# A hybrid decoder trunk on one core: the next block's x rows queued behind late weight loads, and the position bias spread by a copy inside DRAM in three separate hops

## The chip, the cores and the metric

The kernel runs on one core of one Trainium2 chip. The metric is the device time of one execution in microseconds (us). The time before is the median of three runs.

## The reference, cut to what matters

One decoder layer (DEPTH is 1) over 2048 positions of width 1024, in float32:

```python
h = _rmsnorm(x, norm_w[l])                  # needs the row sums of x*x
proj = h @ w_in[l]                          # one projection, columns split to three mixers
y_a = _hgrn2_branch(...)                    # A: gated linear recurrence
y_b = _gated_deltanet_branch(...)           # B: delta rule
y_c = _swa_sink_branch(c_q, c_k, c_v, c_g, sinks[l], bias_blk)   # C: windowed attention
lifted = jnp.einsum('bsnc,ncd->bsnd', ys, w_branch[l])
merged = jnp.sum(sigmoid(gate_logits) * lifted, axis=2)
x = x + merged @ w_out[l]
return _rmsnorm(x, final_norm)
```

`bias_blk` is a table of 128 queries by 256 keys for each of 8 heads. An entry depends on the distance of query and key alone, so one row of 384 values per head, read with a shift of one per query, gives the whole table.

## The kernel before

**Tiling.** `block(s)` treats 512 positions; there are four blocks, s = 0 to 3. Channels lie on the 128 partitions. Each block projects `h` (held as a high part `hH` and a low part `hL`, eight tiles of 128 channels each) with weights that are loaded anew: `load_w` (line 62) loads a 128x512 tile `wraw` by a DMA of SP's queue (L65), ACT rounds it to `wh` (L68), DVE takes the rest `wl` (L69), and `mm_ct` (line 74) does 12 matmuls with it (L80 to L82). Each of the three tiles has four buffers.

**Order of a block.** `unit_a(0)` to `unit_a(3)` (branch A, one head each), with `proj_k` among them; then `unit_b(0)` to `(3)`, with `merge(0)` among them; then `unit_c(0)`, `unit_c(1)`, `merge(1)`, then the norm of the next block, `unit_c(2)`, `unit_c(3)`, `merge(2)` and `output`. A `merge` gates and lifts one branch: 16 loads of `in_wct`, eight of `in_wb`. The units' small matmuls write banks `ps_c` of the tags c0 and c1 (two banks each), the projections banks `ps_d` (four).

**Who orders the work.** The Tile framework's planner puts each engine's instructions into one order ahead of the run: by priority, which is the order in the source, as soon as a planned instruction's inputs and buffers are free. At run time every engine works through its own order. All DMAs here are issued by SP, in one order too. `tc.issue_after(ins)` puts what is written under it behind `ins` on that instruction's own engine; it orders the issue and waits for nothing.

**The next block's norm.** `load_x` (line 102) loads one 128x512 part of `x` into `xs` (two buffers, L105) and ACT sums its squares (L107); eight such parts make a block. `norm_scale` (line 109) adds the sums and takes the power -0.5 on POOL (L111, L94, L95), then for each of four position tiles POOL makes a diagonal `dg` (L116) and PE spreads it to all partitions with `onesP` (L117) into a bank of c0; ACT copies the result to `R` (L119). In the source the loads of block s+1 stand behind `c1(yC)` of block s (lines 775 to 779). Nothing but the two `xs` buffers holds them back, so the planner put them early: at the start of block 0, and at the start of blocks 1 and 2.

**The position bias.** `bias_c` (line 250) is called once, behind `unit_a(0)` of block 0. It loads a table `onehot` (L252) and `relb` (L255), a matmul (L258) makes the row of 384 values for 8 heads on 8 partitions, DVE scales it to `rw` (L260). A DMA writes `rw` to DRAM 128 times, as `scr`, with heads outermost (L261: 8 x 128 x 384 values, 1536 KB). A second DMA reads `scr` with a shift of one value per partition into `bias8` (L263, 1024 KB). `bias8` is first used in `unit_c(0)` of block 0.

**Names in unit_a.** L345 to L348 make the gate `F` and the key `K` from the first projection; `silu2` (L99, L100) makes `Q` from the second; POOL multiplies `Q` and `K` to `prod` (L353), DVE then overwrites `Q` with `Q*F` (L354), which the first level's matmuls (L371) read; POOL makes the products `tots` of F over growing runs (L394).

Of the kernel before, what the change touches and what calls it, by code (L numbers as in the profile page):

```python
# [11 lines left out]
F32 = mybir.dt.float32  # L12
# [8 lines left out]
P = 128  # L21
# [3 lines left out]
NT = TB // P  # L25
# [5 lines left out]
RW = 384  # L31
# [7 lines left out]
def _trunk(tc, S, a, out):  # L39
    nc = tc.nc  # L40
# [6 lines left out]
    dram = ctx.enter_context(tc.tile_pool(name="dram", bufs=1, space=DRAM))  # L47
# [11 lines left out]
    def bank(tag="d", w=None):  # L59
        return ps.tile([P, 512], F32, name="ps_" + tag, tag=tag, bufs=4 if tag == "d" else 2)  # L60

    def load_w(src):
        n = src.shape[-1]
        raw = sb.tile([P, 512], F32, name="wraw", tag="wraw", bufs=WB)
        nc.sync.dma_start(raw[:, :n], src)  # L65
        wh = sb.tile([P, 512], F32R, name="wh", tag="wh", bufs=WB)
        wl = sb.tile([P, 512], F32R, name="wl", tag="wl", bufs=WB)
        A.copy(wh[:, :n], raw[:, :n])  # L68
        V.tensor_tensor(wl[:, :n], raw[:, :n], wh[:, :n].bitcast(F32), op=ALU.subtract)  # L69
        return wh[:, :n], wl[:, :n]  # L70

    last_mm, last_act = [None], [None]

    def mm_ct(p, src, rh, rl, nk):
        for q in range(nk // 4):
            wh, wl = load_w(src[q])
            for k4 in range(4):
                kt = 4 * q + k4
                ks = slice(k4 * P, (k4 + 1) * P)
                T.matmul(p, wh[:, ks], rh[kt], start=(kt == 0), stop=False)  # L80
                T.matmul(p, wh[:, ks], rl[kt], start=False, stop=False)  # L81
                last_mm[0] = T.matmul(p, wl[:, ks], rh[kt], start=False, stop=(kt == nk - 1)).ins  # L82
# [19 lines left out]
    def load_x(s, sq, i, tag="xs"):  # L102
        j, half = i // 2, i % 2
        t = sb.tile([P, TB], F32, name="xs", tag=tag, bufs=2)
        nc.sync.dma_start(t, a["x"][s * TB + j * P:s * TB + (j + 1) * P, half * TB:(half + 1) * TB])  # L105
        scrp = sb.tile([P, TB], BF16, name="scrp", tag="scrp", bufs=1)
        A.activation(scrp, t, AF.Square, accum_out=sq[:, j, half:half + 1])  # L107

    def norm_scale(sq):
        rs = sb.tile([P, NT], F32, name="rsx", tag="rsx")  # L110
        G.tensor_tensor(rs, sq[:, :, 0], sq[:, :, 1], op=ALU.add)  # L111
        rsq(rs, rs, 1.0 / D, EPS)
        rp = bank("c0")
        for j in range(NT):
            dg = sb.tile([P, P], F32, name="dg", tag="vn")
            G.tensor_tensor(dg, ident, rs[:, j:j + 1].broadcast_to([P, P]), op=ALU.mult)  # L116
            T.matmul(rp[:, j * P:(j + 1) * P], onesP, dg, start=True, stop=True)  # L117
        R = sb.tile([P, TB], F32, name="R", tag="R", bufs=1)
        A.copy(R, rp)  # L119
        return rs, R  # L120
# [15 lines left out]
    def mm_tc(src, n, lh, ll, step=1, each=None, tags=("d", "d", "d", "d")):  # L136
        pj = [bank(t) for t in tags]
        for k0 in range(0, KT, step):
            w = []
            for kt in range(k0, k0 + step):  # L140
                if each:
                    each(kt)
                w.append(load_w(src[kt]))
            for j in range(NT):
                js = slice(j * P, (j + 1) * P)
                for kt in range(k0, k0 + step):
                    wh, wl = w[kt - k0]
                    T.matmul(pj[j][:, :n], lh[kt][:, js], wh, start=(kt == 0), stop=False)  # L148
                    T.matmul(pj[j][:, :n], lh[kt][:, js], wl, start=False, stop=False)  # L149
                    T.matmul(pj[j][:, :n], ll[kt][:, js], wh, start=False, stop=(kt == KT - 1))  # L150
        return pj
# [95 lines left out]

    bias8 = const.tile([P, 8, 256], F32, name="bias8", tag="bias8")

    def bias_c():  # L250
        onehot = sb.tile([33, RW], F32, name="onehot", tag="tr", bufs=2)
        nc.sync.dma_start(onehot, a["onehot"])  # L252
        relb = const.tile([33, 8], F32, name="relb", tag="relb")
        G.memset(relb, BIG)
        nc.sync.dma_start(relb[0:32, :], a["relb"])  # L255
        scr = dram.tile([P, 8, RW], F32, name="scr", tag="scr")
        pb = bank("c0")
        T.matmul(pb[0:8, :RW], relb, onehot, start=True, stop=True)  # L258
        rw = sb.tile([8, RW], F32, name="rw", tag="tr", bufs=2)
        V.tensor_scalar(rw, pb[0:8, :RW], 8.0, None, op0=ALU.mult)  # L260
        nc.sync.dma_start(scr.rearrange("p h w -> h p w"), rw.rearrange("h (o w) -> h o w", o=1).broadcast_to([8, P, RW]))  # L261
        skew = bass.AP(tensor=scr.tensor, offset=scr.offset + 127, ap=[[8 * RW - 1, P], [RW, 8], [1, 256]])
        nc.sync.dma_start(bias8, skew)  # L263

    halo = const.tile([P, 12, 3], F32, name="halo", tag="halo")
    G.memset(halo, 0.0)
# [16 lines left out]
    def block(s, hH, hL, last=None):  # L283
# [342 lines left out]
        def proj_k():  # L626
            pk = proj_ct(32)
            for g in range(2):
                r = slice(g * 64, g * 64 + 64)
                if s > 0:  # L630
                    for t in (kH[g], kL[g]):
                        G.tensor_copy(t[:, 0:P], t[:, TB:TB + P].bitcast(F32))
                for r2 in (r, slice(64 - g * 64, 128 - g * 64)):
                    A.copy(kH[g][r2, P:], pk[r, :])
                    V.tensor_tensor(kL[g][r2, P:], pk[r, :], kH[g][r, P:].bitcast(F32), op=ALU.subtract)
# [109 lines left out]
        yA = new_y()  # L745
        f0 = unit_a(0)
        if s == 0:
            bias_c()
        f1 = unit_a(1)
        f0(yA)  # L750
        proj_k()
        f2 = unit_a(2)
        f1(yA)
        f3 = unit_a(3)
        with tc.issue_after(last_act[0]):
# [18 lines left out]
        c1(yC)  # L774
        if s + 1 < NSB:
            sq = sb.tile([P, NT, 2], F32, name="sqx", tag="sqx")
            for i in range(2 * NT):
                load_x(s + 1, sq, i)
            R = norm_scale(sq)[1]
        unit_c(2)(yC)  # L780
        unit_c(3)(yC)
# [5 lines left out]
    for s in range(NSB):  # L787
        hs_ = block(s, *hs_)
# [88 lines left out]
```

## Time and profile before

| | us |
|---|---|
| median of three runs | 2551.77 |
| lowest and highest | 2550.91, 2551.85 |
| the profiled execution, whole | 2551.53 |
| its span, first to last instruction | 2549.7 |

The profiled execution is 0.24 us under the median, and 1.83 us of it lie outside its span. TensorE (PE) is busy for 97% of the span, DVE for 58%, ACT for 45%, POOL for 19%, and the 16 DMA engines for about a third of it. A busy figure is a mean over stages; the stages differ, and what a change in one of them is worth is read from that stage.

A block takes about 628 us, and block 0 has a start of some 45 us ahead of it. PE's clock has two levels in the records, 1.2 and 2.4 GHz; a stretch's granted clock is the mean share of full speed, so 0.83 over 10 us means that 3.4 of them ran at half speed.

### The profile page before, as it was taken

What the parts mean: (1) busy time and instruction counts of PE and PEld (TensorE: products, weight loads), DVE (VectorE), ACT (ScalarE), POOL (GpSimd) and SP (SyncE); (2) the same over time, 40 slices, a digit from 0 to 9 for tenths busy, and PEclk for the clock granted to TensorE, in tenths of its full rate; (3) what the DMA queues carried; (4) which work ended last, traced back from release to release, by engine and by line L of the source; (5) the groups of instructions that cost most, each with busy time, mean ns of one, the idle gap of its engine ahead of it and who ended that gap; (6) DMA issues with size and microseconds to landing.
All of it is one profiled execution on the core that took longest, in us unless ns stands there. A gap on an engine that the chain in (4) does not pass through costs nothing.

```text
span 2549.7 us, 39021 instructions
## 1 busy us (share of the span) xinstructions
PE 2464.3 (97%) x13658; PEld 1945.7 (76%) x13658; DVE 1487.5 (58%) x3706; ACT 1151.0 (45%) x2806; POOL 472.0 (19%) x821
## 2 busy tenths in 40 slices
PE   8899998999999999899999999989999999998998
PEld 7677776778977777677887777767788787776876
DVE  5566566555467657555536666664554676666443
ACT  6354344343545434435444643443434463444343
POOL 3221111211222201120222311111121221111112
PEclk9999999999999999999999999989999999999999
DMA  7423331224522233122452223212344223221233
GB/s 218 79 90 83 84 89 43 66 83 151 164 67 69 78 84 86 43 77 88 147 151 59 78 80 86 80 35 87 91 127 127 63 78 82 84 74 49 83 108 95
DMA packets 162265, 229.97 MB, mean 90 GB/s; under 512 B 49379, under 2 KB 60548, under 8 KB 162068
## 3 DMA queue, kind: packets, MB, share of 16 engines
q1 hardware_dynamic: 162068, 227.47, 31.3%
q8 instruction: 108, 1.77, 0.3%
q14 instruction: 89, 0.73, 0.1%
HBM read 214.53 MB, written 12.88 MB: 89 GB/s over the span
## 4 chain that ended last, share of the span: by engine, by line
PE 87%; DVE 4%; DMA 4%; ACT 2%; POOL 1%; issue 1%; SPq 0%; POOLq 0%; DVEq 0%; ACTq 0%
PE ps_d L80 21%; PE ps_d L81 21%; PE ps_d L82 20%; PE ps_d L149 3%; PE ps_d L148 3%; PE ps_d L150 3%; PE ps_c L371 2%; PE ps_c L701 2%; DMA wraw<-in_wct_dram 1%; PE ps_c L692 1%; DMA scrX<-L 1%; PE ps_c L516 1%; PE ps_c L570 1%; DMA XB<-scrX 1%; DVE wl L69 1%
## 5 line engine op out<-in xcount | busy, mean ns | idle before, releaser
L80 PE MATMUL ps_d<-hH,wh 128*128 128x512 f32 x1952 | 790.8, 405 | 12.3 <-DVE mm L669 5.9
L82 PE MATMUL ps_d<-hH,wl 128*128 128x512 f32 x1952 | 796.4, 408 | 0.1
L68 ACT CAST wh<-wraw 128x512 fp32r<-128x512 f32 (+1 forms) x712 | 429.1, 604 | 812.5 <-PE ps_d L81 659.1
L81 PE MATMUL ps_d<-hL,wh 128*128 128x512 f32 x1952 | 792.0, 406 | 0.0
L69 DVE TENSOR_TENSOR wl<-wraw,wh 128x512 fp32r<-128x512 f32 (+1 forms) x712 | 487.9, 687 | 409.8 <-ACT wh L68 400.0
L80 PEld LDWEIGHTS ps_d<-hH,wh 128*128 128x128 f32 x1952 | 370.9, 190 | 93.2 <-DVE mm L669 6.5
L82 PEld LDWEIGHTS ps_d<-hH,wl 128*128 128x128 f32 x1952 | 370.9, 190 | 79.2 <-issue 1.7
L81 PEld LDWEIGHTS ps_d<-hL,wh 128*128 128x128 f32 x1952 | 370.7, 190 | 79.0 <-issue 0.9
L331 POOL TENSOR_TENSOR msum<-msum,gth 128x512 f32<-128x512 f32 x64 | 104.7, 1638 | 452.1 <-DVE gth L330 452.1
L80 PE MATMUL ps_d<-yH,wh 128*128 128x512 f32 x384 | 154.8, 405 | 3.9 <-ACT yH L311 3.3
L81 PE MATMUL ps_d<-yL,wh 128*128 128x512 f32 x384 | 158.0, 412 | 0.5 <-DVE yL L312 0.5
L82 PE MATMUL ps_d<-yH,wl 128*128 128x512 f32 x384 | 158.1, 412 | 0.0
L148 PE MATMUL ps_d<-wh,mH 128*128 128x512 f32 x256 | 100.1, 391 | 0.0
L149 PE MATMUL ps_d<-wl,mH 128*128 128x512 f32 x256 | 100.0, 391 | 0.0
L150 PE MATMUL ps_d<-wh,mL 128*128 128x512 f32 x256 | 99.9, 390 | 0.0
L471 DVE SCALAR_TENSOR_TENSOR qkB<-raw,convw,qkB 128x512 f32<-128x512 f32 x96 | 71.6, 746 | 29.2 <-ACT qkB L469 28.4
L80 PEld LDWEIGHTS ps_d<-yH,wh 128*128 128x128 f32 x384 | 72.5, 190 | 20.8 <-ACT yH L311 4.1
L81 PEld LDWEIGHTS ps_d<-yL,wh 128*128 128x128 f32 x384 | 73.1, 190 | 19.1 <-DVE yL L312 2.3
L82 PEld LDWEIGHTS ps_d<-yH,wl 128*128 128x128 f32 x384 | 73.1, 190 | 15.3 <-issue 0.3
L330 DVE SCALAR_TENSOR_TENSOR gth<-gth,ps_d 128x512 f32<-128x512 f32 x64 | 43.7, 685 | 68.0 <-PE ps_d L82 67.8
L371 PEld LDWEIGHTS ps_c<-qk 128*64 128x64 f32 x1536 | 53.3, 139 | 38.8 <-issue 20.5
L221 POOL TENSOR_TENSOR soB<-soB,eq 128x1 f32<-128x1 f32 x64 | 15.1, 236 | 346.4 <-ACT junkB L618 346.3
(281 smaller groups left out, 3813.1 us busy)
## 6 DMA issues: line engine op xcount, KB each, us to landing
wraw<-in_wct_dram SPq DMA_DIRECT2D x488, 256.0 KB, 2.6
wraw<-in_wb_dram SPq DMA_DIRECT2D x96, 256.0 KB, 2.6
wraw<-in_wo_dram SPq DMA_DIRECT2D x64, 256.0 KB, 2.6
wraw<-in_wtc_dram SPq DMA_DIRECT2D x64, 162.0 KB, 2.8
xT<-in_xT_dram SPq DMA_DIRECT2D x32, 256.0 KB, 4.2
xs<-in_x_dram SPq DMA_DIRECT2D x32, 256.0 KB, 4.2
rt<-in_x_dram SPq DMA_DIRECT2D x32, 256.0 KB, 3.3
out_dram<-rt SPq DMA_DIRECT2D x32, 256.0 KB, 2.6
```

The lines of the kernel that those rows point to most:

```text
L68: A.copy(wh[:, :n], raw[:, :n])
L69: V.tensor_tensor(wl[:, :n], raw[:, :n], wh[:, :n].bitcast(F32), op=ALU.subtract)
L80: T.matmul(p, wh[:, ks], rh[kt], start=(kt == 0), stop=False)
L81: T.matmul(p, wh[:, ks], rl[kt], start=False, stop=False)
L82: last_mm[0] = T.matmul(p, wl[:, ks], rh[kt], start=False, stop=(kt == nk - 1)).ins
L148: T.matmul(pj[j][:, :n], lh[kt][:, js], wh, start=(kt == 0), stop=False)
L149: T.matmul(pj[j][:, :n], lh[kt][:, js], wl, start=False, stop=False)
L150: T.matmul(pj[j][:, :n], ll[kt][:, js], wh, start=False, stop=(kt == KT - 1))
L331: G.tensor_tensor(m, m, th, op=ALU.add)
L371: T.matmul(sp[g * 64:g * 64 + 64, c * 32:(c + 1) * 32], K[:, c * P + g * 64:c * P + g * 64 + 64], qv[:, c, g * nb // 2:(g + 1) * nb // 2, ...
L471: V.scalar_tensor_tensor(dst, raw[:, j:j + TB], convw[:, ti, j:j + 1], dst, op0=ALU.mult, op1=ALU.add)
L701: T.matmul(ob[hh * 64:hh * 64 + 64, ci * P:(ci + 1) * P], cv_[:, c + b, hh * 64:hh * 64 + 64], pts[ci][:, hh, b, :], start=(b == b0), stop ...
```

## The change

The x rows of the next block are issued behind the weight load written last before them, which is the last one of `merge(1)`. `bias_c` is cut into three: `bias_rows` writes `rw` once to DRAM as `rowd` (12 KB); `bias_spread`, behind `unit_a(1)`, copies `rowd` 128 times to `scr`, from DRAM to DRAM, with the 128 copies outermost and 12 KB in each; `bias_load`, behind `unit_a(2)`, reads the shifted table as before. Each hop is put behind the weight load that was written last.

```diff
     def load_w(src):
...
-        nc.sync.dma_start(raw[:, :n], src)
+        last_ld[0] = nc.sync.dma_start(raw[:, :n], src).ins
...
-    last_mm, last_act = [None], [None]
+    last_mm, last_act, last_ld = [None], [None], [None]
...
-    def bias_c():
+    rowd = dram.tile([8, RW], F32, name="rowd", tag="rowd")
+    scr = dram.tile([P, 8 * RW], F32, name="scr", tag="scr")
+
+    def bias_rows():
         onehot = sb.tile([33, RW], F32, name="onehot", tag="tr", bufs=2)
         nc.sync.dma_start(onehot, a["onehot"])
         relb = const.tile([33, 8], F32, name="relb", tag="relb")
         G.memset(relb, BIG)
         nc.sync.dma_start(relb[0:32, :], a["relb"])
-        scr = dram.tile([P, 8, RW], F32, name="scr", tag="scr")
         pb = bank("c0")
         T.matmul(pb[0:8, :RW], relb, onehot, start=True, stop=True)
         rw = sb.tile([8, RW], F32, name="rw", tag="tr", bufs=2)
         V.tensor_scalar(rw, pb[0:8, :RW], 8.0, None, op0=ALU.mult)
-        nc.sync.dma_start(scr.rearrange("p h w -> h p w"), rw.rearrange("h (o w) -> h o w", o=1).broadcast_to([8, P, RW]))
+        with tc.issue_after(last_ld[0]):
+            nc.sync.dma_start(rowd, rw)
+
+    def bias_spread():
+        with tc.issue_after(last_ld[0]):
+            nc.sync.dma_start(scr, rowd.rearrange("h (o w) -> o (h w)", o=1).broadcast_to([P, 8 * RW]))
+
+    def bias_load():
         skew = bass.AP(tensor=scr.tensor, offset=scr.offset + 127, ap=[[8 * RW - 1, P], [RW, 8], [1, 256]])
-        nc.sync.dma_start(bias8, skew)
+        with tc.issue_after(last_ld[0]):
+            nc.sync.dma_start(bias8, skew)
...
         f0 = unit_a(0)
         if s == 0:
-            bias_c()
+            bias_rows()
         f1 = unit_a(1)
+        if s == 0:
+            bias_spread()
         f0(yA)
         proj_k()
         f2 = unit_a(2)
+        if s == 0:
+            bias_load()
...
         c1(yC)
         if s + 1 < NSB:
             sq = sb.tile([P, NT, 2], F32, name="sqx", tag="sqx")
-            for i in range(2 * NT):
-                load_x(s + 1, sq, i)
+            with tc.issue_after(last_ld[0]):
+                for i in range(2 * NT):
+                    load_x(s + 1, sq, i)
             R = norm_scale(sq)[1]
```

## Rows read from the trace of the kernel before

**Rows 1.** The page: each engine's busy us, share of the span, instructions.

```profile
PE 2464.3 (97%) x13658; PEld 1945.7 (76%) x13658; DVE 1487.5 (58%) x3706; ACT 1151.0 (45%) x2806; POOL 472.0 (19%) x821
```

**Rows 2.** PE's waits over the span: us in total, times, longest.

```profile
PE ps_c L117 <- POOL dg L116: 5.4, 4, 1.9
PE ps_d L80 <- ACT wh L68: 4.1, 1, 4.1
PE ps_c L371 <- DVE qk L354: 3.7, 1, 3.7
```

**Rows 3.** SP's timeline, 75 to 185 us: start, length, then what was issued.

```profile
92.14 0.30 SPq L261 DMA_DIRECT2D scr<-rw  x1
94.30 20.30 SPq L65 DMA_DIRECT2D wraw<-in_wct_dram  x4
```

**Rows 4.** The chain that ended last, 90 to 130 us: start, length, what.

```profile
94.30 31.31 DMA wraw<-in_wct_dram
```

**Rows 5.** PE's timeline, 119 to 131 us; in brackets the idle time before and its releaser.

```profile
126.30 0.60 PE L80 MATMUL ps_d<-hH,wh 128*128 128x512 f32 x1 [4.14 <-ACT wh L68]
126.70 0.63 PE L81 MATMUL ps_d<-hL,wh 128*128 128x512 f32 x1
```

**Rows 6.** Stretches: length, busy time by engine, granted clock, DMA share, GB/s.

```profile
60.00:70.00 10.00, 6.26 (x39) 4.92 (x38) 3.41 (x6) 5.59 (x12) 5.75 (x11) 0.93 0.44 147
70.00:80.00 10.00, 10.00 (x84) 7.04 (x84) 5.84 (x15) 0.62 (x1) 0.00 (x0) 0.73 0.30 81
...
120.00:130.00 10.00, 5.86 (x19) 4.09 (x18) 2.72 (x4) 4.27 (x7) 2.43 (x8) 0.83 0.70 192
...
1030.00:1090.00 60.00, 50.45 (x270) 36.73 (x270) 37.82 (x137) 23.64 (x65) 7.92 (x17) 0.91 0.15 37
...
2286.00:2346.00 60.00, 49.26 (x278) 35.75 (x277) 41.85 (x143) 26.74 (x75) 8.00 (x12) 0.97 0.16 41
...
1280.00:1330.00 50.00, 49.69 (x282) 45.15 (x281) 18.91 (x42) 27.29 (x64) 9.24 (x22) 1.00 0.58 170
```

**Rows 7.** Tile xs, 25 to 66 us: count, ns least/median/most, first to last start.

```profile
L105 SPq DMA_DIRECT2D xs<-in_x_dram x10: 327/328/430, 29.5 to 63.0; - x10
...
L107 ACT ACTIVATION_READ_ACCUMULATOR scrp<-xs x8: 186/187/193, 34.5 to 62.8; 128x1 f32 x8
```

**Rows 8.** POOL's timeline, 58 to 70 us.

```profile
61.97 2.86 POOL L394 TENSOR_TENSOR tots<-tots 128x128 f32<-128x128 f32 x6
65.04 0.20 POOL L111 TENSOR_TENSOR rsx<-sqx 128x4 f32<-128x4 f32 x1 [0.21 <-issue]
...
66.62 1.26 POOL L353 TENSOR_TENSOR prod<-qk 128x512 f32<-128x512 f32 x1
```

**Rows 9.** ACT's timeline, 48 to 70 us.

```profile
55.85 0.63 ACT L107 ACTIVATE scrp<-xs 128x512 bf16<-128x512 f32 x1 [1.34 <-DMA xs<-in_x_dram]
...
59.41 0.60 ACT L345 ACTIVATE F<-ps_d 128x512 f32<-128x512 f32 x1
...
63.38 0.59 ACT L99 ACTIVATE th<-ps_d 128x512 f32<-128x512 f32 x1
```

**Rows 10.** PE's timeline, 64 to 70 us.

```profile
64.61 0.40 PE L82 MATMUL ps_d<-hH,wl 128*128 128x512 f32 x1
68.75 1.07 PE L371 MATMUL ps_c<-qk 128*64 128x32 f32 x16 [3.74 <-DVE qk L354]
```

**Rows 11.** DMAs by kind: line engine op xcount, KB each, median us to landing.

```profile
xs<-in_x_dram SPq DMA_DIRECT2D x32, 256.0 KB, 4.2
...
LT<-gscr SPq DMA_DIRECT2D x16, 256.0 KB, 3.3
```

**Rows 12.** SP's timeline, 484 to 530 us, end of merge(1) in block 0.

```profile
495.43 0.33 SPq L65 DMA_DIRECT2D wraw<-in_wb_dram  x1
498.23 25.53 SPq L65 DMA_DIRECT2D wraw<-in_wct_dram  x10
```

**Rows 13.** PE's timeline, 526 to 529 us: the scores of unit_c(2).

```profile
528.16 0.28 PE L663 MATMUL ps_c<-kH,qs 128*128 128x256 f32 x1
```

## Prediction

> **What bounds the kernel now.** The page comes first: PE is busy for 2464.3 of 2549.7 us [rows 1]. So only three things can move the time much: a gap of PE, a stretch in which PE's clock is at its lower level, or another order of PE's work. I therefore read PE's waits next. Nearly all are short and come back in every block; two are single and long: 4.1 us for a rounded weight, and 3.7 us for `Q*F` [rows 2]. Both lie in the first 130 us, and the change touches what stands ahead of each.
>
> The first: SP issues the write of `scr` at 92.14, and from 94.30 four weight loads behind it [rows 3]. The chain shows a weight load from 94.30 on its way for 31.31 us [rows 4], and PE runs dry 4.14 us before 126.30 [rows 5]. So the write of 1536 KB took some 31 us, 51 GB/s, and the loads that share its queue ended with it. When PE starts again it is at half speed: 0.60 and 0.63 us for matmuls that take 0.40 elsewhere, and a granted clock of 0.83 over 10 us [rows 5, 6, 10].
>
> The second: PE ends its third projection at 65.0 and waits 3.74 us for L354 [rows 10]. POOL is what is late: it ends `tots` at 64.83, then does three norm instructions of block 1, and only at 66.62 `prod` [rows 8], which L354 must await. The norm waits for ACT's squares of x rows; ten row loads are in those first 65 us [rows 7]. So the early rows put 1.8 us into POOL's order, and squares into ACT's ahead of `F` [rows 8, 9]. PE's clock is 0.93 and 0.73 in the two stretches of 10 us around it [rows 6].
>
> **The change part by part.** The sums are against the profiled execution, 2551.53 us, of which 1.83 lie outside the span and don't change; the median is 0.24 higher.
>
> *The bias in three hops.* Removed is the 1536 KB write from eight partitions; added are a 12 KB write, a copy of 1536 KB inside DRAM and one more wait of SP. No copy inside DRAM is in the trace. From below: at the best rate of the stretches shown, 192 GB/s [rows 6], 1536 KB take 8.2 us. From above: six times a broadcast of one DRAM row to 256 KB, at 3.3 us to landing [rows 11], 20 us. I take 10, nearer the lower end, since each of the 3.3 us has a start and an end in it that one copy has once. Loads behind the copy land later by up to that. The load of 94.30 was needed when PE ran dry, at 126.30 - 4.14 = 122.2 [rows 5], less 0.6 for rounding (the size of ACT's step in [rows 9]), so it may take 27 us, and either end fits. The gap goes: -4.1 us. With it goes the slow stretch behind it, 10 x (1 - 0.83) = 1.7 us [rows 6]. SP's added wait, of the 12 KB write to landing, is at most the 3.3 us of a load twenty times its size [rows 11], within the same 27; only weight loads are queued behind it. `bias_load` is the same DMA as before, one unit later; SP again holds loads behind its wait for `scr`, and `bias8` isn't needed before `unit_c(0)`, at the end of branch B. Sum: -5.8 us; between 0 (the cover doesn't reach) and -5.8.
>
> Here the Trainium skill speaks against the step. By "DMA: Bandwidth & Descriptors", section "Rules for kernel authors", an outermost dimension of fewer than 16 confines a DMA to as many engines. By that the old write sat on 8 of them, and the new copy, with 128 outermost, sits on all 16, so that no part of a weight load can pass it. The 51 GB/s of the old write agree; no run here shows the copy yet. The same page's section "Specifications" gives about 358 GB/s of HBM for a core; reading and writing 1536 KB would by that be an estimate of 8.8 us, and the sum is the same.
>
> *The x rows at the start of block 0.* Ten loads of 256 KB leave (block 1's eight and two of block 2's [rows 7]), with eight squares of 0.63 us on ACT [rows 9] and POOL's three norm steps. `prod` needs `Q`: `th` ends at 63.97 [rows 9], DVE's step on it is one of at most 0.87, which is all that lies between the end of `prod` and PE's start [rows 8, 10]; so 64.8, and POOL is free of `tots` at 64.83. With the norm gone `prod` starts at 64.9, 1.75 us earlier, and the gap would still be 2.0. But `F`, `tots` and `th` move too: ahead of `F` ACT waited 1.34 us for an x row, behind a square stands another, and more stand before `th` [rows 9]. If `F` comes 2 to 3 us earlier, `prod` can start at about 62.0 to 62.5 and PE 1.26 + 0.87 later, at 64.1 to 64.6, before the third projection ends at 65.0 [rows 8, 10]. So the gap lies between 0 and 2.0. I take 0, since the square of [rows 9] waited for its x row, and `F` stood in ACT's order behind it. Gain: 3.7 us, and with the gap its slow stretch, 10 x (0.07 + 0.27) = 3.4 us [rows 6]. Sum: -7.1; between -1.8 (POOL's part alone, and the clock falls as now) and -7.1. What is late next is PE itself, which has projections to do.
>
> *The x rows at the start of blocks 1 and 2.* PE is busy for 49.69 of 50 us there [rows 6], so what leaves costs it little: 0 to 1 us in all. I take -0.5.
>
> *The norm in its new place.* The rows now leave behind the load of 495.43 (block 0; the others lie one block apart), in a stretch in which SP loads one projection weight each 2.8 us, ten in 28 us [rows 12], and each pays for 12 matmuls. Eight issues of SP, and on ACT eight squares of 0.63 + 0.19 [rows 7, 9], 6.6 us, beside a share of 45% over the span [rows 1]; nothing by itself. L117 waits for `dg` 5.4 us in four places now, the longest, 1.9, in the start of block 0, which stays [rows 2]; the other three cost 3.5 in sum and leave the end of branch B. In the new place PE reaches L117 with the same POOL steps ahead of it: 0 to 1.9 a block. I take 1.2 each, the mean of those three: net 0; between -3.5 and +2.2.
>
> *The clock in branch C.* The 60 us there have 0.91 in block 1 and 0.97 in block 3, with much the same work but for the norm [rows 6]: 60 x 0.06 = 3.6 us that hang on where short gaps fall. The change shifts them all. I take 0; up to 3.6 us either way in a block, and, as they won't all fall alike, 6 in all.
>
> Sum: -5.8 - 7.1 - 0.5 + 0 = -13.4; 2551.5 - 13.4 = 2538.1 us, its own range 2531 to 2545.
>
> **The rivals.**
> *The start stays half late* (0.14). Only POOL's 1.75 us come off, because `F` waited for PE's first projection and not for ACT's squares, which the trace doesn't tell apart, and the clock still falls: -5.8 - 1.8 - 0.5, so 2543.4.
> *The copy takes the old write's place* (0.08). If it takes over 27 us, or the planner puts it where SP's lead over PE is shorter, PE runs dry as before: -7.1 - 0.5, so 2543.9; with the start half late too, 2549.
> *Nothing that counts moves* (0.09). The planner orders the block anew once x rows aren't ready early; PE's gaps come back at other lines and eat the gain: 2548 to 2554. For it speaks that the two long waits are only 8 us of 85 in which PE idles; against it, that both have a named cause that goes.
> *More than the two gaps* (0.08). The norm takes branch C's gaps and slow stretches along, as block 3 lacks them: 3 x (1.2 + 2.1) more, 2528.
> *The norm comes too late* (0.06), slower than before. R's bank is one of the two c0 banks that `unit_c(2)` needs for its third score matmul, at 528.16 [rows 13]. The last of eight rows is issued at 495.8 + 7p, where p is the pace that SP's order and the two `xs` buffers allow; then 4.2 to land [rows 11], 0.6 for the square, 1.6 for the norm's steps on POOL [rows 8] and 1.9 for `dg` and L117, as its longest wait [rows 2]. That is 504.1 + 7p, in time up to p = 3.4. One row per weight load is p = 2.8, in time by 4 us. At p = 4.5 PE waits 7.5 us in each of three blocks, +22, and the time is 2560. It decides against the change from 3.4 + (13.4 / 3) / 7 = 4.0 us a row.
> The forecast keeps 0.55.
>
> **How the numbers follow.** A change under 0.2%, 5.1 us, can't be told from none here, so faster means under 2546.7: all of the forecast and of "more", nine tenths of the half late start, half of the slow copy, 0.80. Slower is the late norm and a little of "nothing", 0.07. The rest, 0.13, is the same. For 8 in 10 I leave out the late norm, half of "nothing" and what lies under 2526: 2526 to 2551.
>
> **What would show it.** Right, if PE's waits have no row of L80 for L68 and none of L371 over 1 us in the first 130 us, if the stretch from 60 to 80 us has a granted clock of 1.00, if weight loads behind the copy land within 20 us, and if L105 stands behind the last `in_wb` load of `merge(1)`, with L117 in the projections that follow. Wrong, if PE waits over 2 us at L117 or L663 near 500 to 530 us of a block, or if SP's waits show L65 held behind L105 while PE idles for `wh`.

## The result, and the profile after

The changed kernel takes 2525.29 us (median of four, 2522.55 to 2526.73) beside 2551.34 (four, 2545.85 to 2551.85): ratio 0.9896, 95% interval 0.9881 to 0.9911. That is 26 us less, where 13.4 were forecast, and just under the low end of the range, 2526. Four more executions in a later set gave 2525.87 beside 2549.39 (0.991, interval 0.9893 to 0.9928), 23.5 less. The direction and both named causes were right; about half of the gain was not in the sum.

The profiled execution of the changed kernel took 2523.94 us, 2522.2 of it span. Lines behind the bias functions are 10 higher in it (L371 is L381, L353 is L363, L307 is L317). The page's engine totals, as in [rows 1]:

```profile
PE 2450.0 (97%) x13658; PEld 1936.2 (77%) x13658; DVE 1488.5 (59%) x3706; ACT 1153.1 (46%) x2806; POOL 475.8 (19%) x821
```

PE does the same 13658 matmuls in 14.3 us less, and is idle for 72.2 us where it was idle for 85.4. So of 27.5 us of span, 13.2 were idle time and 14.3 were busy time. Most of the latter is clock: span x (1 - granted clock) fell by 13.0, from 33.1 (0.987) to 20.2 (0.992). The forecast had 8.3 of idle time and 5.1 of clock.

PE's waits (total, times, longest) have no row of L80 for L68 and none of L381; of L117 and L317 they say:

```profile
PE ps_c L317 <- ACT LT L315: 6.2, 4, 1.6
...
PE ps_c L117 <- POOL dg L116: 1.8, 3, 1.1
```

L117 fell from 5.4 [rows 2], and L317 rose: it was 3.7 us as L307 of the kernel before. SP's timeline from 75 to 130 us shows the three hops:

```profile
81.42 0.30 SPq L264 DMA_DIRECT2D rowd<-rw  x1
83.58 0.33 SPq L65 DMA_DIRECT2D wraw<-in_wct_dram  x1
83.95 0.58 SPq L268 DMA_DIRECT2D scr<-rowd  x1
86.88 9.47 SPq L65 DMA_DIRECT2D wraw<-in_wct_dram  x2
96.44 0.39 SPq L273 DMA_DIRECT2D bias<-scr  x1
```

The DMAs by kind (count, KB, us to landing) have the copy, and ACT's timeline has the rounding of the load issued behind it at 86.88:

```profile
scr<-rowd SPq DMA_DIRECT2D x1, 1536.0 KB, 8.6
```

```profile
93.33 0.62 ACT L68 CAST wh<-wraw 128x512 fp32r<-128x512 f32 x1 [0.71 <-PE ps_d L81]
```

The copy took 8.6 us, 183 GB/s, where the old write of the same bytes took some 31: [rows 4] show a load queued behind it, and its own packets ran from 93.0 to 124.6. ACT waited for a buffer that PE had to leave, not for the load. Stretches at the start of block 0, with columns as in [rows 6]:

```profile
60.00:70.00 10.00, 10.00 (x108) 7.25 (x107) 6.56 (x17) 1.74 (x3) 0.00 (x0) 1.00 0.30 85
70.00:80.00 10.00, 10.00 (x77) 7.59 (x76) 6.23 (x16) 6.34 (x16) 4.36 (x13) 1.00 0.18 50
...
120.00:130.00 10.00, 10.00 (x119) 7.34 (x116) 8.02 (x20) 3.63 (x9) 0.00 (x0) 1.00 0.16 48
```

PE is full and at its upper clock where it had 0.93, 0.73 and 0.83. POOL (first fence) has no norm step between `tots` and `prod` [rows 8]; `prod` ends at 58.50, and PE (second fence) goes from its third projection to L381 without a gap, at 60.91 instead of 68.75 [rows 10]:

```profile
54.08 2.79 POOL L404 TENSOR_TENSOR tots<-tots 128x128 f32<-128x128 f32 x6
57.20 1.30 POOL L363 TENSOR_TENSOR prod<-qk 128x512 f32<-128x512 f32 x1 [0.33 <-DVE qk L100]
```

```profile
60.59 0.39 PE L82 MATMUL ps_d<-hH,wl 128*128 128x512 f32 x1
60.91 0.66 PE L381 MATMUL ps_c<-qk 128*64 128x32 f32 x16
```

In its new place the norm is in time. SP issues eight rows from 474.59 to 487.6, 1.9 us a row, behind the last `in_wb` load of `merge(1)`; PE takes the four `dg` (L117, eight instructions) within projections. In block 0, shown here, no wait is over 0.1; in blocks 1 and 2 the longest is 0.32, and the three blocks' waits listed above sum to 0.6, for 3.5 before:

```profile
474.21 0.33 SPq L65 DMA_DIRECT2D wraw<-in_wb_dram  x1
474.59 0.90 SPq L105 DMA_DIRECT2D xs<-in_x_dram  x2
...
485.84 2.12 SPq L105 DMA_DIRECT2D xs<-in_x_dram  x2
```

```profile
495.27 0.61 PE L117 MATMUL ps_c<-dg,onesP 128*128 128x128 f32 x4
495.63 0.47 PE L80 MATMUL ps_d<-hH,wh 128*128 128x512 f32 x1
496.19 0.85 PE L117 MATMUL ps_c<-dg,onesP 128*128 128x128 f32 x4
```

**Where the 27.5 us of span lie.** From PE's timeline I take four milestones: the first projection of `hH`, the first matmul of branch B's inversions that reads `X` and `NS`, the first score matmul of branch C, and the first matmul of `output()`. Lengths in us:

| stretch | before | after | change |
|---|---|---|---|
| start to first projection of hH | 47.7 | 43.0 | -4.7 |
| block 0, to branch B | 182.2 | 170.4 | -11.8 |
| block 0, branch C to output | 222.2 | 219.1 | -3.1 |
| block 1 and 2, start to branch B | 240.7, 242.1 | 240.6, 240.7 | -1.5 |
| block 1 and 2, branch C to output | 219.65, 219.95 | 217.3, 217.3 | -5.0 |
| branch B of blocks 0 to 2 | 500.2 | 499.7 | -0.5 |
| block 3 and the end | 675.0 | 674.1 | -0.9 |

The second row holds both forecast gaps, and there the forecast (4.1 + 1.7 + 3.7 + 3.4 = 12.9) was nearly right. The head (-4.7) was in no step, and branch C (-8.1 in this pair) was put at 0. The stretches of branch C, before (first fence) and after; the second column is the length, the third PE's busy time, and the granted clock is third from the end:

```profile
396.60:618.80 222.20, 208.48 (x1027) 161.53 (x1028) 117.50 (x318) 91.99 (x232) 34.51 (x39) 0.96 0.27 77
1026.40:1246.00 219.60, 209.08 (x1052) 162.83 (x1053) 119.11 (x318) 94.08 (x232) 34.99 (x40) 0.97 0.27 78
```

```profile
380.00:599.00 219.00, 207.53 (x1027) 160.68 (x1028) 118.74 (x318) 97.65 (x248) 36.74 (x42) 0.97 0.30 88
1006.30:1223.60 217.30, 206.06 (x1052) 160.36 (x1053) 119.57 (x318) 98.96 (x248) 37.89 (x43) 0.98 0.30 88
```

In block 1 PE's idle time rose by 0.7 us (10.5 to 11.2) and its busy time fell by 3.0 with the same 1052 instructions: there the gain of branch C is clock. In block 0, 2.2 of the 3.1 us were idle time (13.7 to 11.5). What this pair shows does not hold for all traces, as the experiments tell.

The head hangs on POOL. Timelines of POOL before (first fence) and after (second):

```profile
22.97 0.38 POOL L94 TENSOR_SCALAR rsx<-rsx 128x4 f32<-128x4 f32 x1
28.83 0.31 POOL L356 MEMSET ST<- 64x256 f32 x1 [5.48 <-DMA scrX<-zb]
29.22 1.03 POOL L95 TENSOR_TENSOR rsx<-rsx,mhalf 128x4 f32<-128x4 f32 x1
30.33 0.76 POOL L116 TENSOR_TENSOR dg<-ident,rsx 128x128 f32<-128x128 f32 x2
```

```profile
20.61 0.38 POOL L94 TENSOR_SCALAR rsx<-rsx 128x4 f32<-128x4 f32 x1
21.08 1.38 POOL L95 TENSOR_TENSOR rsx<-rsx,mhalf 128x4 f32<-128x4 f32 x1
22.54 1.11 POOL L116 TENSOR_TENSOR dg<-ident,rsx 128x128 f32<-128x128 f32 x2
27.60 0.31 POOL L366 MEMSET ST<- 64x256 f32 x1 [3.96 <-DMA scrX<-zb]
27.99 0.76 POOL L116 TENSOR_TENSOR dg<-ident,rsx 128x128 f32<-128x128 f32 x2
```

In the kernel before, the norm of block 0 stood behind a memset of `ST` (unit_a's, line 356) that waits until the zeros of `zb` have gone to `scrX`; in the changed kernel the planner put that memset behind half of the norm. R is copied 4.5 us after the memset before and 1.7 us after it now (33.30 to 28.83, 29.32 to 27.60). No line of the change touches this memset.

### The profile page after: what moved, and what is told of

It reads as the page before. It is cut to its first block, busy times and chain, and to the rows that moved or that the text cites. A ratio compares the mean times of both kernels' runs of the same rounds, so it can differ in the third digit from the quotient of the medians.

```text
span 2522.2 us, 39006 instructions
## 1 busy us (share of the span) xinstructions
PE 2450.0 (97%) x13658; PEld 1936.2 (77%) x13658; DVE 1488.5 (59%) x3706; ACT 1153.1 (46%) x2806; POOL 475.8 (19%) x821
## 4 chain that ended last, share of the span: by engine, by line
PE 90%; DVE 4%; DMA 2%; ACT 2%; issue 1%; POOL 1%; SPq 0%; POOLq 0%; DVEq 0%; ACTq 0%
PE ps_d L80 21%; PE ps_d L81 21%; PE ps_d L82 21%; PE ps_d L148 3%; PE ps_d L149 3%; PE ps_d L150 3%; PE ps_c L381 2%; PE ps_c L711 2%; PE ps_c L702 1%; DMA scrX<-L 1%; PE ps_c L526 1%; PE ps_c L580 1%; DMA XB<-scrX 1%; PE ps_c L623 1%; PE ps_c L614 1%
## 5 line engine op out<-in xcount | busy, mean ns | idle before, releaser
L80 PE MATMUL ps_d<-hH,wh 128*128 128x512 f32 x1952 | 787.7, 404 | 8.2 <-DVE mm L679 5.9
L68 ACT CAST wh<-wraw 128x512 fp32r<-128x512 f32 (+1 forms) x712 | 429.2, 604 | 798.2 <-PE ps_d L81 621.5
L80 PEld LDWEIGHTS ps_d<-hH,wh 128*128 128x128 f32 x1952 | 368.8, 189 | 88.0 <-DVE mm L679 6.5
L80 PE MATMUL ps_d<-yH,wh 128*128 128x512 f32 x384 | 155.9, 408 | 4.1 <-ACT yH L321 3.7
L148 PE MATMUL ps_d<-wh,mH 128*128 128x512 f32 x256 | 99.9, 390 | 0.0
L80 PEld LDWEIGHTS ps_d<-yH,wh 128*128 128x128 f32 x384 | 72.8, 191 | 21.6 <-ACT yH L321 4.6
L381 PEld LDWEIGHTS ps_c<-qk 128*64 128x64 f32 x1536 | 52.5, 137 | 34.5 <-issue 15.9
```

The source lines that it names most:

```text
L381: T.matmul(sp[g * 64:g * 64 + 64, c * 32:(c + 1) * 32], K[:, c * P + g * 64:c * P + g * 64 + 64], qv[:, c, g * nb // 2:(g + 1) * nb // 2, ...
```

## Experiments

Before a time, "beside" is the kernel before in the same set. Executions of one program scatter by some 4 us (their standard deviation), so a verdict on a time goes by its interval, and the stretches above, from one trace each, stand beside it. Theory: the two parts add; the bias gives its gap and the head, the x rows the start of block 0 and branch C. Rivals: the head's gain comes with the rows; branch C is redrawn by any edit.

**The bias part alone.**

```diff
-            with tc.issue_after(last_ld[0]):
-                for i in range(2 * NT):
-                    load_x(s + 1, sq, i)
+            for i in range(2 * NT):
+                load_x(s + 1, sq, i)
```

> Only the bias in three hops; the x rows as before. Theory (the two parts add; the x rows carry the start of block 0 and branch C): the wait of L80 for L68 is gone, the 3.7 us of the first level's matmuls for Q*F stay, half-speed stretches of branch C stay as before (15 to 16 of 3.4 us behind 400 us). New in its planned order is that POOL's L95 and two dg stand ahead of the memset of ST that waits for the zero write of scrX, so the first projection of hH comes 2 to 4 us earlier than 47.7. Sum -5.8 - 3 = about 2543 (2541 to 2546). Rival 1 (the head's gain hangs on the x rows' transfers): first projection of hH stays at 47 to 48, time 2545.5. Rival 2 (any edit redraws branch C's half-speed stretches): their number behind 400 us changes by 3 or more though nothing there was edited, and the time lies 5 or more from 2543.

2536.36 beside 2549.34, ratio 0.9947 (0.9929 to 0.9966): 13.5 us (8.7 to 18.1), more than twice the forecast 5.8 and past the theory's 2541. No wait of L80 for L68; of Q*F:

```profile
PE ps_c L381 <- DVE qk L364: 3.7, 1, 3.7
```

Block 0 to branch B took 174.7, 7.5 less than before: the 5.8 of the sum and 1.7 of clock behind the Q*F wait. The first projection of hH came at 45.8, so the head's gain doesn't wait for the rows. The time lies 6.6 from the theory, and behind 400 us there are 11 half-speed stretches, counted as the expectation does, for 14 before: both as the second rival asked. Branch C of blocks 0 to 2, 219.1, 218.1 and 219.5, is shorter by 0.5 to 3 each though nothing there was edited. This part carries more than its own gap.

**The x rows alone** (the converse edit of the kernel before).

```diff
-            for i in range(2 * NT):
-                load_x(s + 1, sq, i)
+            with tc.issue_after(last_ld[0]):
+                for i in range(2 * NT):
+                    load_x(s + 1, sq, i)
```

> Only the x rows late; the bias as before. Theory (parts add): the 4.1 us wait for a weight behind the old write stays, with its slow stretch; the wait for Q*F goes (-3.7) with its slow stretch (-3.4); branch C has half-speed stretches as in the changed kernel (10 of 3.4 us behind 380 us for 16 before: -10). POOL's order at the head is as before (memset ahead of L95), so the first projection of hH stays at 46 to 48. About 2534 (2531 to 2537). Rival 1 (the prediction's own sum, branch C not touched by the norm's place): 2544. Rival 2 (the head's gain comes with the x rows): first projection of hH at 43 to 44, 2530.

2535.41 beside 2549.34, 0.9939 (0.9919 to 0.9959): 15.6 us (10 to 21), as the theory had it and twice the prediction's 7.6. PE's waits keep L80 for the old write, and have none of Q*F:

```profile
PE ps_d L80 <- ACT wh L68: 4.1, 1, 4.1
```

Block 0 to branch B took 177.0 (-5.2), the first projection of hH came at 45.4. The two parts sum to 29 by the ratios, the whole change gave 23.5 and 26; within their intervals they add. But branch C was not as expected: 221.4, 220.1 and 218.9 with the norm late (the profiled execution was 10.6 over the median).

**Late rows for block 1 alone, for blocks 2 and 3 alone** (bias as before; the second kernel has `s > 0` where the first has `s == 0`).

```diff
+            with ExitStack() as ord_:
+                if s == 0:
+                    ord_.enter_context(tc.issue_after(last_ld[0]))
                 for i in range(2 * NT):
                     load_x(s + 1, sq, i)
```

> x rows of block 1 alone are queued late (issued in block 0); blocks 2 and 3 get theirs early, and the bias is as before. Theory (each block's norm costs its own branch C; the start of block 0 is worth 7): the wait for Q*F gone, and block 0's branch C loses its half-speed stretches of 423 to 475 us in part; blocks 1 and 2 last 627 and 628.5 as before. -7.1 - 3 to -5: 2540 (2538 to 2543). Rival (the stretches of branch C are redrawn in all blocks by any shift): blocks 1 and 2 change by 2 us or more although nothing of theirs was edited.

> x rows of blocks 2 and 3 alone are queued late (issued in blocks 1 and 2); block 1 gets its rows at the start as before, and the bias is as before. Theory: block 0 as before with both long waits; blocks 1 and 2 shorter by 2.5 and 4.1 as in the changed kernel: 2551.5 - 6.6 = 2545 (2543 to 2547). Rival (the prediction's sum: 0.5 to 1 at the starts, nothing in branch C): 2550.5 to 2551. Rival (redrawn by any shift): block 0 changes by 2 us or more.

2540.71 (0.9966, 0.9952 to 0.998) and 2548.13 (0.9994, 0.998 to 1.0009), beside 2549.34. Block 1's rows carry 8.7 us (5 to 12), as expected; those of blocks 2 and 3 carry 1.5 (-2.3 to 5.1), below the theory's 6.6 and near the prediction's 0.5 to 1. And blocks that nobody edited changed: block 2 by -3.9 in the first kernel, block 0, to output, by +14.5 in the second, of which 10 are PE at half speed near 232 us (a granted clock of 0.74 from 220 to 260). One pair of traces doesn't price branch C.

**The changed kernel again, and shifted.** Two kernels repeat the first matmul of `proj_k` in block 0, which moves all that follows by some 1.6 or 3.2 us (`again` is 4 or 8 there, else 0).

```diff
+                for _ in range(again if kt == 0 else 0):
+                    T.matmul(p, wh[:, ks], rh[kt], start=True, stop=True)
                 T.matmul(p, wh[:, ks], rh[kt], start=(kt == 0), stop=False)
```

> The changed kernel once more, as a measure for the three others of this set. Of each execution two parts are told apart: what the lower clock cost, span x (1 - granted clock), and the rest, span x granted clock. Four executions of it gave 22.7 and 2500.5 in the mean, 23 of the kernel before 34.2 and 2513.4. Theory (part of the gain is how short gaps fall against the clock, the same in every execution of one program): again 20 to 26, and 2525 in all. Rival (it was chance of those four executions): 28 or more, and 2530 or more.

> The changed kernel with proj_k of block 0 doing its first matmul four times more (each begins the sum anew), some 1.6 us of PE work near 150 us, ahead of all of branch B and C. Nothing behind it is edited; each engine's order there is that of the changed kernel but for some 25 places near proj_k. Theory (what the lower clock costs hangs on when the gaps of branch C come, not on how much work or idle time there is): the cost by the lower clock moves by 3 us or more from that of the changed kernel, and the time by that much about 2526.9, up or down. Rival (it hangs on the gaps alone, which the shift leaves as they are): cost by the clock 21 to 25, time 2526.9 (2525.5 to 2528).

> The same with eight matmuls more, some 3.2 us. Theory: the cost by the lower clock need not be that of four more nor of the changed kernel; between 18 and 34. Rival (gaps alone): 21 to 25, time 2528.5 (2527 to 2530).

2525.87, 2529.76 and 2530.08 beside 2549.39. The cost by the clock was 26.5, 29.5 and 26.8 in the mean, but from 20 to 38 between single executions. So the same program's stretches at the lower clock fall otherwise from one execution to the next, and neither theory holds as written: it is no fixed property of the order, and a shift doesn't undo the gain. The kernel before had 34.2 (23 executions), 34.0 (11), 34.5 (17) and 32.9 (25) in the four sets: the fall to 23 to 27 is real, and larger than the 5.1 in the sum.

**The same shift on the kernel before.**

> The kernel before with four matmuls more in proj_k of block 0 (1.6 us), ahead of branch B and C; each engine's order is else as before but for some places near proj_k. Theory (L117's early place costs): branch C as long as before, 218 to 223 in blocks 0 to 2, time 2551 (2549 to 2553). Rival (how the clock falls decides, and the kernel before was unlucky): mean of the three under 218, time 2543 to 2548.

2546.51 beside 2546.88, 0.9996 (0.9981 to 1.001). The time is in the rival's range, but the kernel before stood there too in this set; the shift brought nothing of the size that was missing. Branch C took 220.9, 219.7 and 217.8, mean 219.5: long, as expected of the early place of L117. The kernel before was not merely unlucky.

**PE's part of the norm late, the rest early** (kernel before; the four dg share one tile, so that POOL needn't wait for PE).

```diff
-            dg = sb.tile([P, P], F32, name="dg", tag="vn")
+            dg = dgs[:, j, :] if late else sb.tile([P, P], F32, name="dg", tag="vn")
...
-            T.matmul(rp[:, j * P:(j + 1) * P], onesP, dg, start=True, stop=True)
+            with ExitStack() as behind:
+                if late:
+                    behind.enter_context(tc.issue_after(last_mm[0]))
+                T.matmul(rp[:, j * P:(j + 1) * P], onesP, dg, start=True, stop=True)
```

> The kernel before with PE's part of the next block's norm alone late: rows, squares, rsx and the four dg early as before (the dg now in one tile with room for all four), the four L117 behind the last matmul of merge(1), their place in the changed kernel. POOL does all four dg (1.6 us) ahead of prod, so the wait for Q*F grows from 3.7 to 4.5 to 5.4. From the first score matmul of branch C to the start of output() the traces so far with L117 early have 215.9 to 223.5 us in blocks 0 to 2 (nine blocks, mean 219.7), those with it late 215.3 to 221.4 (18 blocks, mean 217.9). Theory (L117 in branch C's chain of small matmuls costs 1.5 to 2.5 a block): 216 to 218.5 in blocks 0 to 2, time 2546 (2544 to 2548). Rival (its place doesn't count; branch C is shorter in the changed kernel by how the clock falls): 218 or more in the mean, 2550 to 2552.

2545.41 beside 2546.88, 0.9986 (0.9968 to 1.0005). Branch C took 220.85, 218.3 and 215.55, mean 218.2, within the theory's band; the wait for Q*F grew to 4.58, and that of L80 for the old write's load to 5.6 for 4.1, so two waits of block 0 are 2.3 longer, which the time has to carry. The time leans to the theory, but its interval holds no change too. Over all traces, block by block by where the kernel has its L117 (the one in which PE waits for it, below, left out), means:

| branch C to output, us | L117 early | L117 late | no norm |
|---|---|---|---|
| block 0 | 221.6 (5 blocks) | 219.1 (10) | 219.9 |
| blocks 1 and 2 | 218.75 (10) | 217.4 (20) | 215.6, 215.1 |
| block 3, never a norm | 213.8 (17) | | |

The late place saves 2.5 + 2 x 1.35 = 5.2 us; single blocks scatter by 1.5, so it is uncertain by some 1.4. By PE's busy time in these stretches 2.9 of the 5.2 are idle time (13.0 to 11.7 in block 0, 11.0 to 10.2 in blocks 1 and 2) and 2.4 are busy time. Most kernels with L117 late have their rows and squares late too, so the table does not price L117 alone.

**No norm in blocks 1 to 3.** The changed kernel without x rows, squares, `rsx`, `dg` and L117 of these blocks; R of block 0 serves for all.

```diff
-            sq = sb.tile([P, NT, 2], F32, name="sqx", tag="sqx")
...
-            R = norm_scale(sq)[1]
+            R = R0
```

> The changed kernel without the norms of blocks 1 to 3 (no x rows, squares, rsx, dg, L117; block 0's R is used for all blocks): the bound of what the norm costs in its late place. Each engine's order is else the changed kernel's but for a few places. From the first score matmul of branch C to the start of output() it took 217 to 219.5 us in blocks 0 to 2 of the changed kernel, 213 to 214.5 in block 3, which has no norm. Theory (the norm makes that difference): 213 to 215 in all blocks, time 2513 to 2518. Rival (it costs next to nothing in its late place, and block 3 is shorter for another reason): 216 or more, time 2522 to 2525.

2520.73 beside 2549.85, 0.9882 (0.986 to 0.9904). Between the two: beside the changed kernel's 2525.87, from another set, the norm in its late place costs 5 us in three blocks, or 7 by the ratios, uncertain by as much again; the theory's 10 is not excluded by that, but its range of times was missed. Its first two stretches of branch C:

```profile
380.60:600.40 219.80, 208.32 (x1019) 162.13 (x1020) 115.65 (x315) 91.74 (x231) 33.38 (x35) 0.95 0.27 78
1008.00:1223.60 215.60, 205.65 (x1043) 160.48 (x1044) 116.50 (x315) 93.40 (x231) 34.37 (x36) 0.98 0.28 79
```

Block 0's is as long without the norm, at a clock of 0.95: that length is clock, not norm, in this one trace.

**POOL's and PE's part of the norm late, rows and squares early** (kernel before; `last_add` is POOL's last sum of `merge(1)`).

```diff
+            with tc.issue_after(last_add[0]):
-            R = norm_scale(sq)[1]
+                R = norm_scale(sq)[1]
```

> The kernel before with the next block's norm alone late: its POOL and PE steps stand behind POOL's last sum of merge(1), the x rows and ACT's squares stay at the start. Theory (the prediction's: POOL's three steps are 1.8 of the 3.7 us, the squares ahead of F the rest): the wait for Q*F falls to 1.5 to 2.3, its slow stretch stays, 2547 (2544 to 2549). Rival 1 (POOL's steps are all of it): wait under 0.5, 2541 to 2543. Rival 2 (the squares are all of it): 3.3 or more.

2552.89 beside 2549.85, 1.0011 (0.9994 to 1.0028). Two things in PE's waits:

```profile
PE ps_c L117 <- POOL dg L116: 11.7, 4, 3.3
...
PE ps_c L371 <- DVE qk L354: 2.8, 1, 2.8
```

The wait for Q*F fell by 0.9, not by the 1.8 of POOL's three steps: with them gone `prod` stands at 65.27, just behind `tots`, and `tots` waits for `F`. So three quarters of the 3.7 us came from ACT's squares and the rows. And the norm here comes too late: PE waits 3.3 us for `dg` in each of three blocks, the prediction's last rival, with its place (L117 beside `merge(1)`'s end) but by another road, POOL's order and not the rows' pace.

**The old write in the new place.** The changed kernel with the write from eight partitions for the copy; the 12 KB hop falls away, and `rw` stays in SBUF.

```diff
-            nc.sync.dma_start(scr, rowd.rearrange("h (o w) -> o (h w)", o=1).broadcast_to([P, 8 * RW]))
+            nc.sync.dma_start(scr.rearrange("p (h w) -> h p w", h=8), rw_[0].rearrange("h (o w) -> h o w", o=1).broadcast_to([8, P, RW]))
```

> The changed kernel with the old 1536 KB write from eight partitions in place of the copy inside DRAM; all else as changed (x rows late, hops written apart; the write is again followed by four weight loads and then by the load of bias8). Theory (it is the write's form that starves PE): the wait of L80 for L68 is back with 3.5 to 4.5 us and a half-speed stretch behind it; from the first projection of hH to the start of branch B some 5 to 6 us more than in the changed kernel; 2531 to 2534. Rival (it is where the hops stand in SP's order): no wait over 1 us, 2525 to 2528.

2534.06 beside 2549.85, 0.9942 (0.9919 to 0.9964), the high end of the theory; block 0 to branch B took 176.6 for 170.4. The gap is back, in PE's timeline (first fence) and the chain of waits (second), with the duration of [rows 4, 5]:

```profile
118.23 0.50 PE L80 MATMUL ps_d<-hH,wh 128*128 128x512 f32 x1 [4.15 <-ACT wh L68]
```

```profile
86.22 31.31 DMA wraw<-in_wct_dram
```

So it is the form of the write. In the kernel before, the DMA share was 0.50 while the old write ran (columns as in [rows 6]):

```profile
92.00:125.00 33.00, 30.16 (x229) 23.16 (x227) 18.13 (x43) 13.35 (x31) 7.76 (x20) 1.00 0.50 69
```

While the copy ran, from 84 to 93 us in the changed kernel, it was 0.82. By the Trainium skill, "DMA: Bandwidth & Descriptors", section "Rules for kernel authors", an outermost dimension under 16 confines a DMA to at most as many engines; half of the 16 busy with 8 outermost agrees with it. But that is a factor of two at most, and 31 against 8.6 us is 3.6. The rest lies in the packets: the old write's 1024 packets of 1536 bytes took 224 ns each in the mean, the copy's 128 packets of 12 KB took 697 ns, eight times the bytes in three times the time. Whether that comes from the packets' length or from their source (SBUF for one, DRAM for the other) no run separates.

**Three hops written together**, none ordered behind a weight load, in the changed kernel.

```diff
-        with tc.issue_after(last_ld[0]):
-            nc.sync.dma_start(rowd, rw)
...
+        nc.sync.dma_start(rowd, rw)
+        nc.sync.dma_start(scr, rowd.rearrange("h (o w) -> o (h w)", o=1).broadcast_to([P, 8 * RW]))
...
+        nc.sync.dma_start(bias8, skew)
```

> The changed kernel with its three hops written together behind unit_a(0), none ordered behind a weight load; copy form as changed. Every engine's planned order is that of the changed kernel but for SP, where bias8's load stands one weight load earlier. Theory (the form alone counts): no wait of L80 for L68 over 0.5 us, 2523 to 2528. Rival (hops close behind each other starve PE): a wait of 1 us or more near 100 to 130, 2528 to 2531.

One execution, 2528.76: a little over the theory's 2528, but block 0 to branch B took 170.3, as in the changed kernel, with no wait of L80 for L68; the difference lies in the head (44.1 for 43.0) and in branch C and the end. Queueing the hops apart moved one weight load in SP's order and gave nothing that shows.

**The memset behind the norm**, in the changed kernel and in the kernel before (`last_dg` is POOL's last `dg`).

```diff
+            with ExitStack() as after_dg:
+                if s == 0 and h < 2:
+                    after_dg.enter_context(tc.issue_after(last_dg[0]))
-            G.memset(ST[64:P, :, 0:64], 0.0)
+                G.memset(ST[64:P, :, 0:64], 0.0)
```

> The changed kernel with one order more: POOL's memset of ST for the first two heads of block 0 stands behind the four dg of block 0's norm. In the changed kernel it stands between the second and the third, and waits for the zero write of scrX until 27.6, so R is copied at 29.3 and PE waits 1.14 at L117 at 28.4. Theory (the head hangs on this wait, which the bias cut moved past half of the norm by the way the planner's order fell): R at 25 to 27, no wait of PE at L117 over 0.5 there, the first projection of hH 1 to 2.5 us earlier than 43.0, time 2523 to 2524.5 plus or minus what the shift does to the clock. Rival (the head hangs on the loads and on PE's own projections): first projection of hH within 0.5 of 43.0, whatever R does.

> The kernel before with POOL's memset of ST of the first two heads behind the four dg of block 0's norm, and nothing else moved by hand. Theory (the bias cut gave the head some 1.4 us by moving this memset in the planner's order): first projection of hH at 44.5 to 46.5 for 46.7 to 47.7 in four traces with the old order; time 2548 (2546 to 2549.5). Rival (the order of this memset gives nothing while ACT's squares stand in the head): 47 or later, 2549.5 to 2551.

In the kernel before it gave 2542.56 beside 2546.88, 0.9978 (0.996 to 0.9995), 5.6 us by the ratio (1.3 to 10) from one POOL instruction's place: the first projection of hH at 43.2, for 46.1 to 47.7, and the wait for Q*F down too:

```profile
63.89 0.66 PE L374 MATMUL ps_c<-qk 128*64 128x32 f32 x16 [2.77 <-DVE qk L354]
```

In the changed kernel, where half of it had come by itself, it gave 2524.37 beside the 2525.87 of the same set: R at 28.46, not 25 to 27, the first projection at 42.5 for 43.0 and 45.1 in two traces of the changed kernel. It is the lowest median of all kernels with the whole computation, but no difference from the changed kernel that these runs resolve. PE's projections hold the rest, as that run's rival said.

## Why the prediction was wrong in size

The signs that the prediction named for being right came: no wait of L80 for L68, none of L371, a granted clock of 1.00 from 60 to 80 us, the rows behind the last `in_wb` load of `merge(1)`, L117 within projections. What failed is the sum. It had no term for the time ahead of the first projection of hH (4.7 us in the pair, 3 in the mean of the traces), and it put the norm's new place and branch C's clock at net 0, where branch C became shorter by some 5.

- **Bias in three hops, -5.8: right in its own stretch, short by the head.** The gap and its clock went (4.1 + 1.7), and the copy took 8.6 us where 10 was taken between 8.2 and 20. The estimate of 8.8 us by the Trainium skill's "DMA: Bandwidth & Descriptors", section "Specifications", is near the 8.6. That is partly luck: the copy's packets ran for 6.7 of the 8.6 us (85.5 to 92.2), 470 GB/s for reading and writing together, so the rate behind the estimate did not set the time. But the step counted only what SP and PE do with the hops. Cutting `bias_c` also changed the planner's order of POOL far ahead of it, at 23 us. Alone it brought the first projection of hH to 45.8, 1.2 under the mean of five traces with the old order (47.0); the memset wholly behind the norm is worth about 4 us in the kernel before. "The planner orders the block anew" stood among the rivals as a loss only. With the old write in the new place the planner put the memset ahead of L94, with L117 waiting 3.2: the gain is the planner's accident, not the copy's.
- **x rows at the start of block 0, -7.1: right in place, near in size.** The wait and the slow stretch are gone: -5.2 to branch B with the rows alone, -4.3 on top of the bias. Some 1.6 us more lie in the head: the first projection of hH came at 45.4 with block 1's rows late, at 46.1 to 47.7 in five traces with rows and memset as before. The split was wrong: POOL's part was put at 1.75 and measured 0.9. That most of it hung on ACT's squares is why the rival of a half late start (2543.4) did not come.
- **x rows at the start of blocks 1 and 2, -0.5**: -1.5 in this pair, nearly all of it block 2's; the run with late rows there alone gave 1.5 in all. Good enough.
- **The norm in its new place, net 0: wrong.** I took L117's wait as 1.2 a block again; it is 0.32 at the most and 0.6 over the three blocks, for 3.5 before, because SP issues a row each 1.9 us, faster than one per weight load (2.8), and POOL and ACT have room there. The low end, -3.5, was the right one for this wait.
- **The clock in branch C, 0 with 6 either way: low.** With the norm out of branch B's end, branch C is shorter by some 5 us over three blocks, 1.4 either way. In the profiled pair that is mostly time at the lower clock (L317's waits grew by most of what L117's lost); over all traces it is as much idle time as busy time. The run that moves L117 alone leans the same way, but its interval holds no change. The 5 are half of the rival "More than the two gaps" (2528, chance 0.08), the nearest of all forecasts. How much of them is the four matmuls, the gap or the clock between them, the runs don't separate.
- **The sum.** Forecast: idle time -8.3, clock -5.1. Measured in the profiled pair: -13.2 of idle time and -14.3 of busy time. The runs put 23.5 to 26 at about 12 for the start of block 0, 3 to 5 for the head, 5 for branch C and 1 to 1.5 for the starts of blocks 1 and 2, 21 to 23.5. What is left, up to 5 us, is of the size by which single sets differ.
- **The chances.** Faster had 0.80 and came. The range missed by 0.7 us: its low end had the norm's and branch C's gain only together, as a rival of 0.08, and nothing for the head, which stood in no term.
- **A reading.** "Two are single and long" passes over a third, longer wait: 6.8 us of L148 for L68 at the very start. It is 6.8 in the changed kernel too, so the sum doesn't hang on it.

## What to carry to other kernels

A DMA's price hangs on its form: the same 1536 KB took 31 us written from eight partitions and 8.6 us copied with 128 rows outermost, in packets eight times as long, and the loads that share its queue pay the difference. Work hoisted far ahead by its free buffers costs on every engine that must do it in order, so price all of its steps where they were, above all those that stand ahead of the longest chain. Where a planner orders the engines, look at each engine's order from its first instruction on, not only around the edit: one memset that waits for a DMA, placed ahead of a norm, was worth about as much as a named gap.

## What was not expected of the hardware

One program's time at the lower clock is not fixed: in 23 executions of the kernel before it cost 28 to 43 us (span x (1 - granted clock)), and their times spread over 17 us; in another set of 25 it cost 23 to 46. Part of a loss can be given back, where a gap behind slow work shrinks: PE's timeline at the same two matmuls of block 1, in the changed kernel (first fence) and in its later execution (second):

```profile
1065.50 0.73 PE L80 MATMUL ps_d<-yH,wh 128*128 128x512 f32 x2 [1.02 <-ACT yH L321]
```

```profile
1064.84 1.22 PE L80 MATMUL ps_d<-yH,wh 128*128 128x512 f32 x2 [0.64 <-ACT yH L321]
```

The second runs at half speed (1.22 for 0.73), as does the score matmul ahead of it (0.41 for 0.28), after a wait shorter by 0.38. So the clock read from one trace is a sample; that its mean fell, by 11.5 us in the first set and 7.5 in the later one, showed only over many executions.
